# A causal convolution module: the sixth chunk's sum moved behind the eighth chunk's gate, the normalisation's diagonal moved to VectorE, projection copies moved between normalised chunks, and the first norm's squares moved behind its operands

## The chip, the cores and the metric

The kernel runs on one NeuronCore of one Trainium2 chip. The core has a matrix engine (TensorE, PE in the profile; its weight loads are PEld), a vector engine (VectorE, DVE), a scalar engine (ScalarE, ACT), a general engine (GpSimd, POOL), and a queue engine (SyncE, SP) that only starts DMA transfers here. Each engine works through its own list of instructions in order; semaphores tie the lists together. The metric is the time of one execution on the device in microseconds (us), as a median of several executions.

## The reference

Two decoder layers on 512 tokens of width 1024. The change touches only the mixer of the first layer, a causal convolution module, and the norm ahead of it:

```python
def rms_norm(x, g):
    xf = x.astype(jnp.float32)
    y = xf * lax.rsqrt(jnp.mean(xf * xf, axis=-1, keepdims=True) + EPS)
    return (y * g.astype(jnp.float32)).astype(x.dtype)

def conformer_conv(x, w_pw1, b_pw1, dw_w, dw_b, ln_g, ln_b, w_pw2, b_pw2):
    a = x @ w_pw1 + b_pw1
    u = a[..., :D_MODEL] * jax.nn.sigmoid(a[..., D_MODEL:])
    u = lax.conv_general_dilated(u, dw_w[:, None, :], ..., padding=[(30, 0)],
                                 feature_group_count=D_MODEL) + dw_b
    u = jax.nn.silu(layer_norm(u, ln_g, ln_b))
    return u @ w_pw2 + b_pw2
```

The rest of the first layer (a gated feed-forward network and a gated per-layer embedding `gate * (p @ w_proj)`) and the second layer (differential attention, the same two again) are unchanged. One thing of the rest is computed early: the product `p @ w_proj` of the first layer fills PE at the end of the convolution.

## The kernel before

Everything is kept transposed: 1024 features are 8 chunks of 128 partitions, and the 512 tokens run along the free axis, so a tile is 128x512. The input chunks are `h0` to `h7`. Every float32 operand of a matrix product is split into a rounded high part and the low rest, and each product is three matmuls (`mm3`, L164 to L166: low x high, high x low, high x high). A weight tile (`weight`, L146) is loaded by SP, its high part copied on ScalarE (L157), its low part made on VectorE (L159).

*The norm ahead (class `Norm`, L181).* `operands(c)` makes the split operand of a chunk: the high part on ScalarE (L178), the low part on VectorE (L179). `squares(c)` squares the chunk on ScalarE (L200, L203) and adds it on VectorE (L204). `columns` sums over the partitions with four narrow matmuls (L210); the reciprocal root is a power on POOL (L229); `diagonal` puts it on a diagonal (L234, VectorE); `spread` (L244) multiplies that by ones, so that each partition holds the row of scales, which ScalarE copies to `rb` (L219). The products are made of the unscaled operands and scaled behind.

*A chunk of the convolution (loop over c, L459 on).* `half` multiplies by the gate half and the other half of the weights, 24 matmuls each. VectorE scales both by `rb` (L478, L484), ScalarE takes the sigmoid (L479), VectorE joins them (L488 or L496). Then come the 31 taps. Chunks 1, 3, 5 and 6 (counted from 0; `PHASED`) take them all on PE: the joined chunk goes to DRAM and back in another layout (`pi`, L333, L337), PE multiplies by prepared matrices (L370), ScalarE copies the result (L378), it goes to DRAM (`po`, L380, from ScalarE's queue) and back (L383, SP), and VectorE adds bias and the common shift `shrow` (L389). This last step I call the chunk's sum. The other chunks take their taps on VectorE (L419, L421), with some on POOL (L409, products by ScalarE, L408) and, for the eighth chunk (c = 7), eight on PE (L326); VectorE joins the parts (L422, L424). `moments(c)` squares a finished chunk on ScalarE (L444) and adds square and chunk to running sums (L448, L450), on POOL up to the sixth chunk, on VectorE for the seventh. The sum of the seventh chunk is kept back (`late`) until the eighth is done.

*The end.* `factor` makes one of eight chunks of `p @ w_proj`, twelve matmuls (L164 to L166, on `wth`, `wtl`) and a copy on ScalarE (L291). `add_moments` sums squares and values over the partitions (L456) and spreads the mean (L457). Four tiny VectorE operations make the variance (L538 to L227), POOL takes the power, the diagonal is made by four scaled copies on ScalarE (L544), PE spreads it (L547). Each chunk is then shifted by the mean (L555 on VectorE for three, L557 on POOL for five), scaled (L564, VectorE), put through SiLU (L565, ScalarE) and split (L567 ScalarE, L569 VectorE). `linear` multiplies by the second weights, with three output chunks in turn to begin with; L593 adds the result to `h`.

The order on each engine is not written out by hand. A scheduler places the instructions by their dependencies, with its own estimate of times; `tc.issue_after(x)` keeps an instruction behind another one, and `tc.manual_schedule` keeps the written order on the engines that it names. So one move in the code shifts neighbours on all engines.

## Time and profile before

| | |
|---|---|
| median of 3 runs | 1267.42 us (1265.94 to 1268.1) |
| the profiled execution | 1268.78 us |
| its span | 1267.0 us |
| PE busy | 1244.6 us, 98% |
| VectorE, ScalarE, POOL busy | 903.4, 614.7, 263.3 us |
| PE's granted clock, mean | 0.992 of full |

The profile is of one execution. "Busy" counts the time in which an engine carries out an instruction. A row of the timeline gives start, duration, engine, line, operation, the tiles written and read, the shape, and in square brackets the idle time ahead of it with what ended that. Neighbouring instructions of one kind are one row (x16), so its duration is that of all. Matmuls overlap, so the distance of their starts tells more than their durations. The granted clock is what PE's throttle let through, 1.00 being full speed.

### The profile page before, as it was taken

What the parts mean: (1) busy time and instruction counts of PE and PEld (TensorE: products, weight loads), DVE (VectorE), ACT (ScalarE), POOL (GpSimd) and SP (SyncE); (2) the same over time, 40 slices, a digit from 0 to 9 for tenths busy, and PEclk for the clock granted to TensorE, in tenths of its full rate; (3) what the DMA queues carried; (4) which work ended last, traced back from release to release, by engine and by line L of the source; (5) the groups of instructions that cost most, each with busy time, mean ns of one, the idle gap of its engine ahead of it and who ended that gap; (6) DMA issues with size and microseconds to landing.
All of it is one profiled execution on the core that took longest, in us unless ns stands there. A gap on an engine that the chain in (4) does not pass through costs nothing.

```text
span 1267.0 us, 18622 instructions
## 1 busy us (share of the span) xinstructions
PE 1244.6 (98%) x7152; PEld 1089.2 (86%) x7152; DVE 903.4 (71%) x1482; ACT 614.7 (49%) x1023; POOL 263.3 (21%) x231
## 2 busy tenths in 40 slices
PE   9999899999999999999999999999999999999998
PEld 7888678888899889988888978778898999899887
DVE  6997765975588558667678869845965588558665
ACT  6742464542355335456566757734542355235442
POOL 2852522000000000042516633122000000000030
PEclk9999999999999999999999989999999999999999
DMA  7665123474466444243222214213464467444241
GB/s 296 195 194 178 58 68 115 124 184 124 120 176 180 127 124 121 63 145 100 87 93 75 76 42 123 94 51 115 131 162 138 111 175 188 141 105 117 82 133 67
DMA packets 60597, 158.39 MB, mean 125 GB/s; under 512 B 6451, under 2 KB 11059, under 8 KB 60508
## 3 DMA queue, kind: packets, MB, share of 16 engines
q1 hardware_dynamic: 53776, 136.99, 34.3%
q0 software_dynamic: 4608, 16.78, 8.1%
q10 hardware_dynamic: 2124, 3.43, 0.9%
q8 instruction: 56, 0.92, 0.3%
q14 instruction: 33, 0.27, 0.1%
HBM read 151.91 MB, written 4.21 MB: 123 GB/s over the span
## 4 chain that ended last, share of the span: by engine, by line
PE 87%; DVE 6%; DMA 2%; ACT 2%; issue 1%; POOL 1%; SPq 0%; DVEq 0%; ACTq 0%; POOLq 0%
PE mm L164 24%; PE mm L165 24%; PE mm L166 24%; PE tp L166 2%; PE tp L165 2%; PE tp L164 2%; PE sc L165 1%; PE sc L166 1%; PE sc L164 1%; DVE wlo L159 1%; POOL wk L409 1%; DMA po<-big 1%; PE sc L370 1%; PE mm L1006 1%; DVE sc L421 1%
## 5 line engine op out<-in xcount | busy, mean ns | idle before, releaser
L165 PE MATMUL mm<-A,whi 128*128 128x512 f32 (+1 forms) x904 | 311.8, 346 | 1.0 <-DVE A L569 0.7
L164 PE MATMUL mm<-A,wlo 128*128 128x512 f32 (+1 forms) x904 | 308.0, 345 | 3.5 <-ACT A L178 1.8
L166 PE MATMUL mm<-A,whi 128*128 128x512 f32 (+1 forms) x904 | 310.2, 344 | 0.0
L157 ACT CAST whi<-wraw 128x1024 fp32r<-128x1024 f32 (+2 forms) x150 | 151.1, 1015 | 224.5 <-PE mm L166 98.5
L159 DVE TENSOR_TENSOR wlo<-wraw,whi 128x1024 fp32r<-128x1024 f32 (+2 forms) x147 | 185.1, 1262 | 58.4 <-ACT whi L157 58.1
L164 PEld LDWEIGHTS mm<-A,wlo 128*128 128x128 f32 x904 | 171.4, 190 | 25.0 <-ACT A L178 2.7
L165 PEld LDWEIGHTS mm<-A,whi 128*128 128x128 f32 x904 | 171.9, 190 | 22.1 <-issue 1.2
L166 PEld LDWEIGHTS mm<-A,whi 128*128 128x128 f32 x904 | 171.9, 190 | 21.0 <-issue 1.4
L165 PE MATMUL mm<-B,whi 128*128 128x512 f32 x368 | 143.9, 392 | 0.0
L166 PE MATMUL mm<-B,whi 128*128 128x512 f32 x368 | 143.8, 392 | 0.0
L164 PE MATMUL mm<-B,wlo 128*128 128x512 f32 x368 | 141.6, 393 | 0.0
L675 POOL DMA_DIRECT2D C<-in_wts x32 | 28.1, 880 | 511.8 <-DVE h L786 179.0
L204 POOL TENSOR_TENSOR acc<-acc,wk 128x512 f32<-128x512 f32 x35 | 56.4, 1610 | 218.1 <-ACT wk L203 110.7
L166 PEld LDWEIGHTS mm<-B,whi 128*128 128x128 f32 x368 | 69.5, 189 | 15.0
L166 PE MATMUL mm<-whi,A 128*128 128x512 f32 (+1 forms) x224 | 82.0, 367 | 0.0
L164 PEld LDWEIGHTS mm<-B,wlo 128*128 128x128 f32 x368 | 69.5, 189 | 14.3
L165 PEld LDWEIGHTS mm<-B,whi 128*128 128x128 f32 x368 | 69.4, 189 | 14.3
L165 PE MATMUL mm<-wlo,A 128*128 128x512 f32 (+1 forms) x224 | 81.6, 367 | 0.0
L164 PE MATMUL mm<-whi,A 128*128 128x512 f32 (+1 forms) x224 | 81.6, 370 | 0.0
L786 DVE TENSOR_TENSOR h<-mm,h 128x512 f32<-128x512 f32 x48 | 33.0, 687 | 64.6 <-PE mm L166 64.4
L229 POOL TENSOR_TENSOR r<-v,mhalf 128x8 f32<-128x8 f32 (+1 forms) x31 | 45.4, 1465 | 118.4 <-DVE v L227 93.1
L668 DVE TENSOR_TENSOR wlo<-wraw,whi 128x1024 fp32r<-128x1024 f32 x32 | 39.2, 1224 | 31.5 <-ACT whi L667 31.4
(271 smaller groups left out, 2674.2 us busy)
## 6 DMA issues: line engine op xcount, KB each, us to landing
wraw<-in_wts SPq DMA_DIRECT2D x162, 512.0 KB, 3.6
C<-in_wts SPq DMA_DIRECT2D x32, 512.0 KB, 4.8
C<-in_wts POOLq DMA_DIRECT2D x32, 512.0 KB, 6.1
bias<-in_wts SPq DMA_DIRECT2D x32, 256.0 KB, 3.4
wraw<-in_wts SPq DMA_DIRECT2D x16, 384.0 KB, 3.1
D<-in_diag SPq DMA_DIRECT2D x22, 256.0 KB, 4.5
C<-in_diag SPq DMA_DIRECT2D x16, 256.0 KB, 4.7
h<-in_xT SPq DMA_DIRECT2D x8, 256.0 KB, 5.5
```

The source lines that it names most:

```text
L157: A.copy(hi[:, cut], raw[:, cut])
L159: eng.tensor_tensor(lo[:, cut], raw[:, cut], f(hi[:, cut]), ALU.subtract)
L164: T.matmul(acc, al, bh, start=first, stop=False)
L165: T.matmul(acc, ah, bl, start=False, stop=False)
L166: return T.matmul(acc, ah, bh, start=False, stop=last)
L204: self.last = self.eng.tensor_tensor(self.acc, self.acc, sq, ALU.add)
L229: last_pow[0] = G.tensor_tensor(r[:, :n], v[:, :n], mhalf[:, :n], ALU.pow)
L370: last_tap[0] = T.matmul(acc[:, g * P : (g + 1) * P], w, ups[c][:, g, LEAD - m : LEAD - m + P], start=(m == 0), stop=(m == LAGS - 1),)
L409: G.tensor_tensor(pacc, pacc, pr, ALU.add)
L668: V.tensor_tensor(lo, raw, f(hi), ALU.subtract)
L675: nc.gpsimd.dma_start(q, wts[i + 2].rearrange("p (a s) -> p a s", a=2), accum_op=ALU.add)
L786: V.tensor_tensor(h[m], acc, h[m], ALU.add)
```

## The change

Five edits, all in the convolution module or the norm ahead of it:

1. `norm.squares` of all eight chunks go behind the last operand's high part. In the second chunk's gate half, the matmuls of the last four input chunks go behind the column sums; its other half goes behind the spread. The two splits of `p` (L278, L279) go behind the power.
2. The sixth chunk's sum (c = 5) is kept back like the seventh's, until the eighth chunk's gate is joined, and its two additions to the running sums go from POOL to VectorE.
3. The fourth `factor` goes from ahead of the moments to behind them: three, moments, two, spread, three, instead of four, moments, one, spread, three.
4. The diagonal is made by one VectorE product (`diagonal`, as in the norms) instead of four ScalarE copies. The tile `drow` for POOL's shifts is made as soon as the mean is there; VectorE's first shift goes behind the variance, the second and third between the scalings.
5. The low parts of the normalised chunks follow one chunk behind instead of two. The last three `factor` calls stand between the first three normalised chunks on ScalarE. The third weight of `linear` no longer waits for the second scaling.

```diff
-    for c in range(NC):
-        norm.squares(c)
+    with tc.issue_after(norm.scaled.ins):
+        for c in range(NC):
+            norm.squares(c)
...
-    def half(w):
+    def half(w, behind=None, first=0):
         acc = mm()
         for k in range(NC):
-            mm3(acc, wpart(w, k), norm.u[k], k == 0, k == NC - 1)
+            with tc.issue_after(behind.ins) if behind and k >= first else nullcontext():
+                mm3(acc, wpart(w, k), norm.u[k], k == 0, k == NC - 1)
...
-        if c < NC - 2:
+        if c < NC - 3:
             late.pop()()
...
-        eng = G if c < NC - 2 else V
+        eng = G if c < NC - 3 else V
         eng.tensor_tensor(sums["acc"], sums["acc"], sq, ALU.add)
...
-            ph = pfeatures(0, [(sb([P, S], t, 2, F32R), sb([P, S], t, 2, F32R)) for t in ("wth", "wtl")])
+            with tc.issue_after(last_pow[0].ins):
+                ph = pfeatures(0, [(sb([P, S], t, 2, F32R), sb([P, S], t, 2, F32R)) for t in ("wth", "wtl")])
...
-            pg = half(wg)
+            pg = half(wg, norm.summed if c == 1 else None, NC // 2)
...
-            pa = half(wa)
+            pa = half(wa, last_spread[0] if c == 1 else None)
...
-            V.scalar_tensor_tensor(up[:, PAD:], ta, col("b_pw1", c), tg, ALU.add, ALU.mult)
+            gate = V.scalar_tensor_tensor(up[:, PAD:], ta, col("b_pw1", c), tg, ALU.add, ALU.mult)
+        if c == NC - 1:
+            with tc.issue_after(gate.ins):
+                late.pop(0)()
...
-    factor(last_product)
     with tc.issue_after(last_product[0].ins):
         add_moments(y[NC - 1], square, True, False)
         add_moments(macc, sums["acc"], False, True)
-    factor(last_moment)
+    for _ in range(2):
+        factor(last_moment)
+    drow = wk()
+    A.mul(drow, sums["mean"], -1.0 / D)
...
-    dg = wk()
-    for b in range(4):
-        A.activation(dg[:, b * P : (b + 1) * P], ident, AF.Copy, scale=r[:, b : b + 1])
+    shift = lambda c: V.scalar_tensor_tensor(y[c], sums["mean"], -1.0 / D, y[c], ALU.mult, ALU.add)
+    with tc.issue_after(last_v[0].ins):
+        shift(0)
+    dg = diagonal(r)
...
-    for _ in range(3):
-        factor(last_product)
     with tc.issue_after(last_pow[0].ins):
-        drow = wk()
-        A.mul(drow, sums["mean"], -1.0 / D)
-        for c in range(NC):
-            if c < 3:
-                V.scalar_tensor_tensor(y[c], sums["mean"], -1.0 / D, y[c], ALU.mult, ALU.add)
-            else:
-                G.tensor_tensor(y[c], y[c], drow, ALU.add)
+        for c in range(3, NC):
+            G.tensor_tensor(y[c], y[c], drow, ALU.add)
...
-        for c in range(NC + 2):
+        for c in range(NC + 1):
             if c < NC:
-                scaled.append(V.tensor_tensor(y[c], y[c], lrow, ALU.mult))
+                if c in (1, 2):
+                    shift(c)
+                V.tensor_tensor(y[c], y[c], lrow, ALU.mult)
...
+                if c < 3:
+                    factor(last_product)
-            if c >= 2:
-                V.tensor_tensor(z[c - 2][1], y[c - 2], f(z[c - 2][0]), ALU.subtract)
+            if c >= 1:
+                V.tensor_tensor(z[c - 1][1], y[c - 1], f(z[c - 1][0]), ALU.subtract)
...
-    linear(NC, z, add_conv, 3, first=(None, last_add[0], scaled[1]))
+    linear(NC, z, add_conv, 3, first=(None, last_add[0], None))
```

What the scheduler makes of it is shown at three places. The changed kernel's line numbers are up to 12 higher than those of the kernel before.

VectorE around the eighth chunk's gate, before. `B_210` is the sixth chunk, `C_225` the eighth behind its gate, `sc_1253` its tap sum, `B_240` the finished eighth chunk:

```order
L421 SCALAR_TENSOR_TENSOR sc_847<-C_159_794,C_24_125,sc_847 128x512 x7
L422 TENSOR_TENSOR B_187_920<-sc_847,wk_888 128x512
L478 TENSOR_TENSOR big_1193<-mm_1090,rb_252 128x512
L159 TENSOR_TENSOR wlo_1464<-wraw_1462,whi_1463 128x1024
...
L389 SCALAR_TENSOR_TENSOR B_210_1080<-B_210_1080,vec_63,shrow_189 128x512
L484 TENSOR_TENSOR big_1194<-mm_1115,rb_252 128x512
L496 SCALAR_TENSOR_TENSOR C_225_1200<-big_1194,vec_63,big_1193 128x512
L419 SCALAR_TENSOR_TENSOR sc_1253<-C_225_1200,C_24_125,shrow_189 128x512
L421 SCALAR_TENSOR_TENSOR sc_1253<-C_225_1200,C_24_125,sc_1253 128x512 x14
L422 TENSOR_TENSOR B_240_1252<-sc_1253,wk_1229 128x512
```

The same place now:

```order
L426 SCALAR_TENSOR_TENSOR sc_847<-C_159_794,C_24_125,sc_847 128x512 x6
L427 TENSOR_TENSOR B_187_920<-sc_847,wk_888 128x512
L484 TENSOR_TENSOR big_1192<-mm_1089,rb_252 128x512
L159 TENSOR_TENSOR wlo_1461<-wraw_1459,whi_1460 128x1024
...
L490 TENSOR_TENSOR big_1193<-mm_1114,rb_252 128x512
L502 SCALAR_TENSOR_TENSOR C_225_1199<-big_1193,vec_63,big_1192 128x512
L394 SCALAR_TENSOR_TENSOR B_210_1080<-B_210_1080,vec_63,shrow_189 128x512
L424 SCALAR_TENSOR_TENSOR sc_1253<-C_225_1199,C_24_125,shrow_189 128x512
L455 TENSOR_TENSOR acc_190<-acc_190,B_210_1080 128x512
L426 SCALAR_TENSOR_TENSOR sc_1253<-C_225_1199,C_24_125,sc_1253 128x512 x3
L453 TENSOR_TENSOR B_93_381<-B_93_381,wk_1272 128x512
L426 SCALAR_TENSOR_TENSOR sc_1253<-C_225_1199,C_24_125,sc_1253 128x512 x11
```

The sixth chunk's sum (L389, now L394) has moved behind the gate, but still stands ahead of the taps, and two additions stand among the taps. The fifth chunk's last run of taps has six where it had seven (the other one stands earlier).

ScalarE at the head, before (`h_7` to `h_14` are the eight input chunks, `A` their operands):

```order
L157 CAST whi_96<-wraw_95 128x512
L178 ACTIVATE A_19_105<-h_7_86,vec_63 128x512
L200 ACTIVATE acc_94<-h_7_86 128x512
L157 CAST whi_96<-wraw_95 128x512
L157 CAST whi_110<-wraw_109 128x512
L178 ACTIVATE A_25_127<-h_8_87,vec_63 128x512
L203 ACTIVATE wk_168<-h_8_87 128x512
```

and now:

```order
L157 CAST whi_96<-wraw_95 128x512
L178 ACTIVATE A_19_105<-h_7_86,vec_63 128x512
L157 CAST whi_96<-wraw_95 128x512
L157 CAST whi_110<-wraw_109 128x512
L178 ACTIVATE A_25_127<-h_8_87,vec_63 128x512
L157 CAST whi_110<-wraw_109 128x512
L178 ACTIVATE A_27_131<-h_9_88,vec_63 128x512
```

The squares have left the places between the operands; they follow the eighth operand.

ScalarE at the end, before (`D`, `C_270` are projection chunks, `B_93`, `B_115`, `B_140` the first three chunks, `A_274`, `A_276` their high parts):

```order
L291 COPY D_259_1323<-mm_1324 128x512
L157 CAST whi_1475<-wraw_1474 128x1024
L291 COPY D_261_1350<-mm_1351 128x512
L544 ACTIVATE wk_1367<-ident_65,r_265_1365 128x128 x4
L552 ACTIVATE wk_1400<-tp_1288 128x512
L291 COPY D_268_1374<-mm_1375 128x512
L565 ACTIVATE B_93_381<-B_93_381,vec_63 128x512
L291 COPY C_270_1383<-mm_1384 128x512
L567 CAST A_274_1414<-B_93_381 128x512
L565 ACTIVATE B_115_536<-B_115_536,vec_63 128x512
L291 COPY C_270_1383<-mm_1392 128x512
L157 CAST whi_1578<-wraw_1577 128x1024
```

and now:

```order
L546 ACTIVATE wk_1359<-tp_1288 128x512
L295 COPY D_259_1341<-mm_1342 128x512
L157 CAST whi_1472<-wraw_1471 128x1024
L295 COPY D_261_1350<-mm_1351 128x512
L571 ACTIVATE B_93_381<-B_93_381,vec_63 128x512
L573 CAST A_269_1383<-B_93_381 128x512
L295 COPY D_271_1386<-mm_1387 128x512
L571 ACTIVATE B_115_536<-B_115_536,vec_63 128x512
L573 CAST A_273_1398<-B_115_536 128x512
L295 COPY C_275_1401<-mm_1402 128x512
L157 CAST whi_1575<-wraw_1574 128x1024
L571 ACTIVATE B_140_652<-B_140_652,vec_63 128x512
```

The four scaled copies are gone, the copy of the mean stands earlier, and each of the last three projection copies stands behind a normalised chunk's high part.

11 lines of the change are left out of this document (6 added, 5 removed).

## The prediction

> **What bounds the kernel now.** I read the page first: how busy is TensorE (PE), and where is it not?
>
> ```profile
> span 1267.0 us, 18622 instructions
> PE 1244.6 (98%) x7152; PEld 1089.2 (86%) x7152; DVE 903.4 (71%) x1482; ACT 614.7 (49%) x1023; POOL 263.3 (21%) x231
> ```
>
> PE is idle for 22.4 us in all. The windows, by 20 us and finer, show where the convolution's share lies (the stretch and its length, then the busy time of PE, weight loads, VectorE, ScalarE and POOL, then PE's granted clock, DMA share and GB/s):
>
> ```profile
> 60.00:80.00 20.00, 20.00 (x115) 17.19 (x114) 19.18 (x23) 9.18 (x13) 7.06 (x7) 1.00 0.61 176
> 140.00:160.00 20.00, 16.51 (x76) 12.29 (x75) 12.95 (x20) 8.07 (x16) 8.69 (x7) 0.91 0.14 39
> ...
> 8.00:12.00 4.00, 4.00 (x12) 3.10 (x12) 4.00 (x7) 3.95 (x8) 0.00 (x0) 0.57 1.06 401
> ...
> 156.00:158.00 2.00, 2.00 (x7) 1.52 (x6) 2.00 (x4) 0.00 (x0) 2.00 (x2) 0.50 0.00 0
> ...
> 700.00:750.00 50.00, 47.60 (x284) 42.09 (x283) 41.09 (x114) 34.95 (x85) 26.40 (x26) 0.93 0.25 74
> ```
>
> In the convolution there are two holes: the head, where the clock was 0.57 of full from 8 to 12 us, and 140 to 165 us, its end, where it fell to 0.50. (The last row is in the attention, where PE waits as well.) In between PE is full (20.00 of 20), and VectorE (19.18) nearly so. What ends the waits of the second hole is in PE's timeline (the last row is from the chain of waits, an earlier spread at full clock):
>
> ```profile
> 143.97 0.50 PE L164 MATMUL mm<-wth,wlo 128*128 128x512 f32 x1 [1.64 <-DVE B L424]
> 145.47 0.95 PE L456 MATMUL tp<-ones,wk 128*128 128x1 f32 x8
> 150.67 0.48 PE L164 MATMUL mm<-wth,wlo 128*128 128x512 f32 x1
> 154.15 1.47 PE L547 MATMUL tp<-wk,ones 128*128 128x512 f32 x2 [1.85 <-ACT wk L544]
> 158.32 0.39 PE L165 MATMUL mm<-wth,whi 128*128 128x512 f32 x1
> 160.61 0.39 PE L166 MATMUL mm<-wtl,whi 128*128 128x512 f32 x1
> 162.49 0.50 PE L165 MATMUL mm<-A,whi 128*128 128x512 f32 x1 [0.70 <-DVE A L569]
> ...
> 28.10 0.86 PE tp L244 x2
> ```
>
> PE waits 1.64 us for the eighth chunk's sum (L424), 1.85 for the diagonal that ScalarE makes (L544), 0.70 for the first normalised chunk. At full clock a matmul starts every 0.229 us (158.32 to 160.61, ten steps); from 154.15 to 158.32 it does one spread and seven matmuls, which at that pace are 0.86 + 7 x 0.229 = 2.46 us: the half clock behind the 1.85 us wait costs 1.7. The output projection, had it not waited, would stand at 162.49 less its three first matmuls, 161.80. That mark is what the change must pull in; behind it PE is the bound, so the end follows it.
>
> What makes L424 late is in VectorE's timeline (the first row is PE's, the first tap of the seventh chunk, which follows the last matmul of the eighth chunk's halves):
>
> ```profile
> 123.16 3.06 PE L370 MATMUL mm<-C,D 128*128 128x128 f32 x26
> ...
> 127.16 1.12 DVE L389 SCALAR_TENSOR_TENSOR B<-B,vec,shrow 128x512 f32<-128x512 f32 x1 [4.64 <-DMA B<-po]
> 128.19 0.68 DVE L484 TENSOR_TENSOR big<-mm,rb 128x512 f32<-128x512 f32 x1
> 128.91 1.33 DVE L496 SCALAR_TENSOR_TENSOR C<-big,vec,big 128x512 f32<-128x512 f32 x1
> 131.14 11.05 DVE L421 SCALAR_TENSOR_TENSOR sc<-C,C,sc 128x512 f32<-128x512 f32 x14
> 142.43 0.69 DVE L422 TENSOR_TENSOR B<-sc,wk 128x512 f32<-128x512 f32 x1 [0.24 <-POOL wk L409]
> 143.23 0.69 DVE L424 TENSOR_TENSOR B<-mm,B 128x512 f32<-128x512 f32 x1
> ```
>
> VectorE stands 4.64 us until the sixth chunk's rows land, and the eighth chunk's gate (L484, L496) stands behind that wait though PE had its input ready at 123.2.
>
> **The change part by part.**
>
> *Head.* ScalarE loses the square between the first operand and the next weight copies:
>
> ```profile
> 5.36 0.62 ACT L200 ACTIVATE acc<-h 128x512 f32<-128x512 f32 x1
> 7.78 1.03 PE L164 MATMUL mm<-A,wlo 128*128 128x512 f32 x2 [0.76 <-ACT A L178]
> 18.75 1.93 DVE L159 TENSOR_TENSOR wlo<-wraw,whi 128x1024 fp32r<-128x1024 f32 x1 [0.30 <-ACT whi L157]
> 19.73 0.95 PE L210 MATMUL tp<-ones,acc 128*128 128x1 f32 x8
> 25.67 1.23 DVE L159 TENSOR_TENSOR wlo<-wraw,whi 128x1024 fp32r<-128x1024 f32 x1 [2.12 <-ACT whi L157]
> 29.61 0.69 DVE L478 TENSOR_TENSOR big<-mm,rb 128x512 f32<-128x512 f32 x1 [2.72 <-ACT rb L219]
> ```
>
> That brings the operand for which PE waits at 7.78 forward by most of 0.62; I take 0.5. From 8 us on PE waits for no operand (4.00 of 4 busy), so the other squares' place only gives slack. The eight squares and their sums are the old instructions in a new order; with the weight splits among them both engines were through at 18.75 + 1.93 = 20.7. The column sums now stand twelve matmuls (2.75 us) further, at 19.2 + 2.75 = 22.0, so they wait for nothing. The row scale is spread after twelve more, at 22.0 + 0.8 + 2.75 = 25.5; with 0.86 for the spread and about 0.7 for the copy behind it, VectorE's first gate starts near 27.1 instead of 29.61. One weight split (1.23, at 25.67 inside that wait) moves behind it, so VectorE is about 1.3 us ahead from there. PE needs that split only for the third chunk, a whole chunk later. On POOL the two splits of the projection's input go behind the first power, which would cost them if POOL had other work; its next is a tap of the first chunk, after the gate. On SP's queue a load for the FFN falls back behind the second chunk's matrices, which nobody waits for; otherwise neighbours change places.
>
> *Sixth chunk's rows.* Their trip begins with a copy on ScalarE behind the fifth chunk's square, which waits for VectorE:
>
> ```profile
> 116.65 0.69 DVE L422 TENSOR_TENSOR B<-sc,wk 128x512 f32<-128x512 f32 x1
> 117.91 0.57 ACT L378 COPY big<-sc 128x512 f32<-128x512 f32 x1
> ```
>
> If VectorE keeps its 1.3 us and has one tap fewer ahead of L422 (the order shows six for seven), the rows land up to 2 us earlier. If the fourth chunk's trip, whose copy now stands one product later, eats it, 0. I take 1.0, the middle.
>
> *Eighth chunk.* Off the path from landing to L424: L484 and L496, 128.91 + 1.33 - 128.19 = 2.05, which run in the former wait, and POOL's 0.24, since its taps start with the gate; together 2.29. On it: the two additions of the sixth chunk to the running sums (L450, L448), which come from POOL to VectorE. Their price alone, then the prices of two operations next to POOL (L569 and L389; L389 alone is above) and that of taps of two chunks in turn:
>
> ```profile
> 146.02 0.69 DVE L450 TENSOR_TENSOR acc<-acc,B 128x512 f32<-128x512 f32 x1
> 160.82 1.62 DVE L569 TENSOR_TENSOR A<-B,A 128x512 fp32r<-128x512 f32 x1 [0.73 <-ACT A L567]
> 84.51 4.04 DVE L421 SCALAR_TENSOR_TENSOR sc<-C,C,sc 128x512 f32<-128x512 f32 x6
> 93.70 2.02 DVE L389 SCALAR_TENSOR_TENSOR B<-B,vec,shrow 128x512 f32<-128x512 f32 x1 [1.38 <-DMA B<-po]
> ```
>
> Alone two adds are 1.38. Taps of one chunk follow each other at 11.05 / 14 = 0.79, taps of two chunks in turn at 4.04 / 6 = 0.67, so an add between two taps gets 0.12 back, 0.24 in all. Next to POOL's seven taps, which now start some 4 us earlier, they could cost 1.62 each, and L389 2.02 instead of 1.12. So this segment changes by -2.29 + 1.38 - 0.24 = -1.15 to -2.29 + 3.24 - 0.24 + 0.90 = +1.6. I take +0.2, the middle, since neither row is nearer: POOL works through all of it, but not always in the same microsecond. L424 then ends at 143.92 - 1.0 + 0.2 = 143.12.
>
> *Moments.* The fourth projection no longer stands ahead of them. They start when the eighth chunk is squared:
>
> ```profile
> 143.95 0.64 ACT L444 ACTIVATE wk<-B 128x512 f32<-128x512 f32 x1 [1.00 <-DVE B L424]
> ```
>
> That is 0.67 after L424: 143.79. PE is free at 143.97 - 1.64 - 0.5 = 141.83, so it waits 1.96. The moments take 150.67 - 145.47 = 5.20 and end at 148.99 (call it E).
>
> *Diagonal and spread.* The four scaled copies (L544) become one VectorE product, priced as an equal one at 22.86:
>
> ```profile
> 151.69 1.02 POOL L229 TENSOR_TENSOR r<-v,mhalf 128x4 f32<-128x4 f32 x1 [9.29 <-DVE v L227]
> 22.86 0.69 DVE L234 TENSOR_TENSOR wk<-ident,r 128x512 f32<-128x512 f32 x1 [1.98 <-POOL r L229]
> ```
>
> POOL's power ends at 152.71, E + 2.04; the diagonal at E + 2.8 (VectorE does the first shift while POOL works). PE meanwhile has two projections, 12 x 0.229 = 2.75. The 1.85 us wait is thus covered, up to 0.6 if POOL's shifts double the diagonal's price. Spread 0.86 and three projections 4.12 bring the output projection to E + 7.78 = 156.77. Gain against 161.80: 5.0 us.
>
> *Normalised chunks.* They pass VectorE and ScalarE in turn:
>
> ```profile
> 160.68 0.82 ACT L565 ACTIVATE B<-B,vec 128x512 f32<-128x512 f32 x1
> 162.81 0.62 ACT L567 CAST A<-B 128x512 fp32r<-128x512 f32 x1
> ```
>
> The first one's low part is due at E + 2.04 + 0.69 (diagonal) + 1.23 (the third weight's split, now ahead of it) + 0.69 (product) + 0.82 (SiLU) + 0.62 + 0.69 (difference) = E + 6.8, with hand-overs some E + 7.3; next to POOL the two-input ones would take it to about E + 8.9. PE comes to it two matmuls into the output projection, at E + 8.2. I charge 0.3, bounds 0 and 0.7. The projection copies, now later on ScalarE, free PE's banks for the second and third weight about an instruction ahead of need.
>
> *Clock.* A wait of 1.64 cost no clock, one of 1.85 cost 1.7 us. The new wait of 1.96 is near that edge: 0 to 1.7, and I take 0.85. [...]
>
> **Sum.** 5.0 - 0.3 - 0.85 = 3.9 us. The profiled execution (1268.78, 1267.0 of it span) becomes 1264.9. It was 1.36 above the median; from the median 1267.42 I predict 1263.5. Two medians closer than 0.2%, 2.5 us, count as the same here.
>
> **The rivals.**
>
> *The new sums are dear.* POOL stays beside VectorE for both adds and L389 (+1.6) and the rows land no earlier. The rows of L569 and L389 next to POOL speak for it; against it, an add may meet a gap between POOL's taps. The moments start at 143.92 + 1.6 + 0.67 = 146.19 after a wait of 4.4, the clock drops (1.7), E = 153.09, the mark 161.17 with 0.3: gain 0.6, 1266.8. [...]
>
> [...]
>
> *Head without half clock.* Less waiting before 8 us may spare the drop there: 4 x (1 - 0.57) = 1.7 more, 1261.8. Nothing in the trace says which.
>
> *Given back later.* Attention has PE waits too, and shifted times may cost one more stretch at half clock: 3.9 - 1.7 = 2.2, 1265.2, about on the 0.2% line.
>
> *Slower: the sixth chunk's rows land late.* All fifteen taps of the eighth chunk stand on VectorE behind L389, so each us of landing beyond 126.2 is a us at the end. The fourth chunk's trip began, in the chain, at
>
> ```profile
> 83.18 0.57 ACT big L378
> ```
>
> The rival decides from 3.9 us late (130.1); at 133, 6.8 late, the kernel takes 1270.3. For it: the trip passes ScalarE's copy, a store, and SP's queue behind the matrix loads. Against: from its copy to VectorE's L389 the fourth chunk's trip took 93.70 - 83.18 = 10.5 and the sixth's 127.16 - 117.91 = 9.3, a spread of 1.2, not 7.
>
> **How the numbers follow.** Forecast 0.42; clock held 0.14; head without half clock 0.09; dear sums 0.19; given back 0.10, half to either side of the line; late rows 0.06. Faster 0.42 + 0.14 + 0.09 + 0.05 = 0.70; same 0.19 + 0.05 = 0.24; slower 0.06. The range runs from the head case with 1 us of the sixth chunk's bound, 1260.8, to the dear sums, 1266.8.
>
> **What would show it.** In the changed profile: the eighth gate starts near 123 and its C tile is written before the sixth chunk's rows land; the wait for the eighth chunk's sum is 1 to 3 us and no longer behind a fourth projection; no wait of 1.85 at the spread; the output projection begins near 156.8. I am wrong if VectorE's adds there take over 1.3 us each, if PE's clock halves for over 4 us, or if a new wait stands ahead of the output projection's second or third weight.

## The result, and the profile after

The changed kernel takes 1272.27 us (median of 7 executions, 1269.98 to 1273.69), the kernel before beside it 1267.42 (7 executions): a ratio of 1.0036, 95% interval 1.0025 to 1.0047. It is 4.9 us slower where 3.9 us less was forecast, and lies outside the range. Measured again on another chip it took 1273.12 us, 1.0030 of the kernel before (1.0010 to 1.0051). Three executions below took 1.6 to 5 times as long as all others (3172.59 us of the kernel before, 6719.67 of *adds on GpSimd*, 2059.47 of *wait filled, shifts behind*): the medians count them, the ratios leave them out.

Lines behind the edits have moved: L389 is now L394, L419 to L424 are L424 to L429, L444 to L457 are L449 to L462, L484 and L496 are L490 and L502. The profiled execution took 1269.98 us, the shortest of the seven. The head came out as forecast. These are the column sums, the spread, ScalarE's copy of the row and VectorE's first gate:

```profile
21.58 0.95 PE L211 MATMUL tp<-ones,acc 128*128 128x1 f32 x8
25.80 1.10 PE L247 MATMUL tp<-wk,ones 128*128 128x512 f32 x2 [0.39 <-DVE wk L235]
26.94 0.59 ACT L220 COPY rb<-tp 128x512 f32<-128x512 f32 x1 [6.84 <-PE tp L247]
27.56 0.69 DVE L484 TENSOR_TENSOR big<-mm,rb 128x512 f32<-128x512 f32 x1 [1.90 <-ACT rb L220]
```

22.0, 25.5 and 27.1 were forecast for the sums, the spread and the gate, and they started at 21.58, 25.80 and 27.56. The next place did not come out so. ScalarE's queue, with the sixth chunk's copy and its store:

```profile
116.54 0.57 ACT L383 COPY big<-sc 128x512 f32<-128x512 f32 x1
119.13 0.33 ACTq L385 DMA_DIRECT2D po<-big  x1
119.55 1.05 ACT L157 CAST whi<-wraw 128x1024 fp32r<-128x1024 f32 x1 [2.44 <-DMA C<-pi]
```

The copy is 1.4 us earlier than before (117.91), yet the store stands 2.0 us behind its end: the profile names a DMA, `C<-pi`, the seventh chunk's reload, as what the cast behind the store, and so ScalarE's queue, waited for. The records of the trace show the tie between the two: store and reload raise the same completion semaphore, the reload's last piece landed at 119.05, and the store started at 119.13. (In the kernel before, 118.58 and 118.66.) So the rows land 0.53 us later than before. VectorE from the eighth chunk's gate to its last sum, and then the diagonal:

```profile
122.99 0.69 DVE L490 TENSOR_TENSOR big<-mm,rb 128x512 f32<-128x512 f32 x1
123.72 0.75 DVE L502 SCALAR_TENSOR_TENSOR C<-big,vec,big 128x512 f32<-128x512 f32 x1
127.69 1.85 DVE L394 SCALAR_TENSOR_TENSOR B<-B,vec,shrow 128x512 f32<-128x512 f32 x1 [3.22 <-DMA B<-po]
129.46 1.73 DVE L424 SCALAR_TENSOR_TENSOR sc<-C,C,shrow 128x512 f32<-128x512 f32 x1
131.10 1.76 DVE L455 TENSOR_TENSOR acc<-acc,B 128x512 f32<-128x512 f32 x1
132.78 2.33 DVE L426 SCALAR_TENSOR_TENSOR sc<-C,C,sc 128x512 f32<-128x512 f32 x3
135.01 0.86 DVE L453 TENSOR_TENSOR B<-B,wk 128x512 f32<-128x512 f32 x1
135.80 8.66 DVE L426 SCALAR_TENSOR_TENSOR sc<-C,C,sc 128x512 f32<-128x512 f32 x11
144.56 0.69 DVE L427 TENSOR_TENSOR B<-sc,wk 128x512 f32<-128x512 f32 x1
145.36 0.69 DVE L429 TENSOR_TENSOR B<-mm,B 128x512 f32<-128x512 f32 x1
...
157.78 1.77 DVE L235 TENSOR_TENSOR wk<-ident,r 128x512 f32<-128x512 f32 x1 [0.55 <-POOL r L230]
```

The gate runs inside the wait for the rows, as forecast. But next to POOL's taps the sum, the first tap and the first addition take 1.85, 1.73 and 1.76 us, where the kernel before had 1.12 and 0.76 for the first two and 0.69 alone for such an addition. The second addition, beside the same taps, takes only 0.86. From landing to the end of the last sum it is 18.36 us against 16.76. PE's waits at the end of the convolution:

```profile
146.77 1.87 PE L461 MATMUL tp<-ones,wk 128*128 128x1 f32 x8 [4.80 <-ACT wk L449]
...
154.82 1.03 PE L461 MATMUL tp<-ones,acc 128*128 128x1 f32 x8
159.70 1.10 PE L559 MATMUL tp<-wk,ones 128*128 128x512 f32 x2 [1.02 <-DVE wk L235]
164.74 0.62 PE L164 MATMUL mm<-A,wlo 128*128 128x512 f32 x2
```

PE waits 4.80 us for the eighth chunk, where the kernel before waited 1.64. The moments, 5.20 us before, last from 146.77 to 155.71, 8.94 us. The windows show why (as before: busy times, then the granted clock):

```profile
140.61:144.03 3.42, 1.35 (x6) 0.78 (x5) 3.28 (x5) 1.18 (x2) 0.00 (x0) 1.00 0.00 0
144.03:147.44 3.41, 0.67 (x4) 0.67 (x4) 3.20 (x5) 0.97 (x2) 0.00 (x0) 0.50 0.00 0
147.44:150.85 3.41, 3.41 (x15) 3.25 (x16) 1.96 (x3) 0.28 (x1) 0.00 (x0) 0.50 0.42 127
150.85:154.27 3.42, 3.42 (x8) 1.52 (x6) 0.00 (x0) 0.27 (x1) 0.00 (x0) 0.50 0.07 26
154.27:157.68 3.41, 3.41 (x23) 3.09 (x24) 1.25 (x5) 0.65 (x2) 0.95 (x1) 1.00 0.00 0
```

The clock is at half for 10.24 us, three stretches of 3.41. The output projection starts at 164.74, 2.94 later than the mark of before. These 2.94 are 1.30 (moments begin later) + 3.74 (moments longer) - 2.10 (from their end to the output projection: 9.03 against 11.13).

### The profile page after: what moved, and what is told of

It is laid out like the page before. It is cut to its first block, busy times and chain, and to the rows that moved or that the text cites. A ratio compares the mean times of both kernels' runs of the same rounds, so it can differ in the third digit from the quotient of the medians.

```text
span 1268.2 us, 18626 instructions
## 1 busy us (share of the span) xinstructions
PE 1243.5 (98%) x7152; PEld 1088.4 (86%) x7152; DVE 909.2 (72%) x1485; ACT 614.5 (48%) x1019; POOL 264.1 (21%) x229
## 4 chain that ended last, share of the span: by engine, by line
PE 81%; DVE 8%; issue 6%; ACT 2%; POOL 2%; DMA 1%; ACTq 0%; SPq 0%; POOLq 0%; DVEq 0%
PE mm L164 22%; PE mm L165 22%; PE mm L166 22%; PE tp L166 2%; PE tp L165 2%; PE tp L164 2%; DVE wlo L159 1%; POOL wk L414 1%; DVE sc L426 1%; PE sc L165 1%; PE sc L166 1%; PE sc L164 1%; PE mm L1014 1%; DVE C L951 1%; DVE big L990 0%
## 5 line engine op out<-in xcount | busy, mean ns | idle before, releaser
L159 DVE TENSOR_TENSOR wlo<-wraw,whi 128x1024 fp32r<-128x1024 f32 (+2 forms) x147 | 185.9, 1267 | 60.8 <-ACT whi L157 60.6
```

The source lines that it names most:

```text
L159: eng.tensor_tensor(lo[:, cut], raw[:, cut], f(hi[:, cut]), ALU.subtract)
```

## The experiments

Theory 1, from the two traces: the eighth chunk's chain is longer, mostly by the two sums on VectorE next to POOL's taps, and the longer wait that follows costs TensorE's clock in the moments. Rival 1: the loss lies in the diagonal on VectorE and the normalised chunks. Rival 2: it lies behind the convolution.

Every kernel was timed in five rounds beside the kernel before (its medians 1266.35 to 1266.86), in 12 executions each, *fourth projection ahead* in six. Four chips were used: one for the second to fifth row of the table, one for the next four, one for the first row and the three of the small fill, one for the last four. So kernels of different chips are compared by their ratios, not by their microseconds. The matmuls that fill waits are extra work that nothing reads. "Clock" is the mean granted clock over the executions; the kernel before had 0.995 (0.989 to 0.998), the changed one 0.992 in both measurements.

| kernel | us | ratio to before | clock, lowest |
|---|---|---|---|
| changed, again | 1273.12 | 1.0030 (1.0010 to 1.0051) | 0.992, 0.989 |
| sums back | 1267.23 | 1.0003 (0.9990 to 1.0016) | 0.994, 0.990 |
| wait filled | 1267.51 | 1.0005 (0.9996 to 1.0015) | 0.996, 0.993 |
| fourth projection ahead | 1274.43 | 1.0049 (1.0034 to 1.0064) | 0.991, 0.989 |
| only the sums | 1271.21 | 1.0032 (1.0019 to 1.0046) | 0.992, 0.989 |
| adds on GpSimd | 1267.06 | 1.0005 (0.9989 to 1.0021) | 0.993, 0.988 |
| the same, both waits filled | 1267.09 | 1.0005 (0.9995 to 1.0016) | 0.996, 0.995 |
| before, waits filled | 1268.07 | 1.0006 (0.9993 to 1.0020) | 0.996, 0.994 |
| wait filled, shifts behind | 1266.38 | 0.9995 (0.9981 to 1.0010) | 0.996, 0.990 |
| adds, small fill | 1268.77 | 1.0015 (0.9997 to 1.0033) | 0.993, 0.989 |
| the same, shifts behind | 1269.49 | 1.0007 (0.9989 to 1.0025) | 0.993, 0.990 |
| the same, store free | 1267.97 | 1.0010 (0.9992 to 1.0028) | 0.994, 0.990 |
| adds, wide fill | 1266.51 | 0.9996 (0.9983 to 1.0008) | 0.996, 0.993 |
| row first, filled | 1264.77 | 0.9984 (0.9972 to 0.9997) | 0.994, 0.992 |
| row first | 1264.74 | 0.9985 (0.9972 to 0.9997) | 0.994, 0.992 |
| row first, store free | 1265.12 | 0.9992 (0.9978 to 1.0005) | 0.993, 0.990 |

**Which part costs it.** *Sums back*, from the changed kernel:

```diff
-        if c < NC - 3:
+        if c < NC - 2:
             late.pop()()
...
-        eng = G if c < NC - 3 else V
+        eng = G if c < NC - 2 else V
...
-        if c == NC - 1:
-            with tc.issue_after(gate.ins):
-                late.pop(0)()
```

> The changed kernel with one part taken back: the sixth chunk's sum stands ahead of the eighth chunk's gate again and its two running sums are on GpSimd. Theory 1 (the eighth chunk's chain and the clock behind it): the two sums cost VectorE about 1.6 us next to GpSimd's taps, and the moments lose 3.7 us at half clock because TensorE waits 4.80 us ahead of them. Here the eighth chunk's last sum should end near 144.4 us instead of 146.05, the wait should be near 3.1 us, and the time should fall by 1.6 us if the half clock stays and by up to 5.3 us if the shorter wait keeps the clock: 1267.0 to 1270.7 us against 1272.3. Rival 1 (the loss lies in the diagonal on VectorE and the normalised chunks): the last sum's end moves but the output projection gains at most 1.6 us. Rival 2 (the loss lies behind the convolution): the output projection starts earlier, and the whole time stays at 1272.

1267.23 us, a ratio of 1.0003 in place of 1.0036 and 1.0030: some 3.4 to 4.2 us of the loss are gone, inside theory 1's range. The loss of clock is rarer here, not gone. Six of 12 executions reach a clock of 0.995, against six of 19 of the changed kernel. The profiled one is this kernel's slowest (1272.37): its stretch from landing to last sum is 16.98 us, PE waits 3.28, and four stretches at half clock follow.

```profile
146.29 1.05 PE L461 MATMUL tp<-ones,wk 128*128 128x1 f32 x8 [3.28 <-ACT wk L449]
```

*Only the sums* is the kernel before with the opposite edit and nothing else:

> The kernel before with one part of the change alone: the sixth chunk's sum behind the eighth's gate and its two running sums on VectorE. Theory 1: the eighth chunk's last sum ends 1.6 us later than in the kernel before (143.9), near 145.5; TensorE waits near 3.2 us instead of 1.64; with the full clock kept the time rises by 1.6 us, with the clock lost by up to 5 us: 1269 to 1272.5 against 1267.4. Rival 1: this part costs nothing by itself: 1267.4, or up to 2 us less since the gate no longer waits.

1271.21 us: this part alone makes the loss, 1.0032 against the whole change's 1.0030 and 1.0036. Its mean clock is 0.992 against 0.995, and 0.003 of 1268 us is 3.8 us, nearly all of the loss. Rival 1 falls; so does rival 2 as a cause, since no code behind the convolution differs here. The other edits together are worth about nothing as they stand. In its trace the stretch from landing to last sum is 18.49 us, but the rows landed at 125.54, so the wait came out at 2.12, not 3.2. It stands right ahead of the moments, as in the changed kernel, although the fourth projection was not moved in the code: the scheduler now has PE do it ahead of the wait.

```profile
144.74 1.05 PE L456 MATMUL tp<-ones,wk 128*128 128x1 f32 x8 [2.12 <-ACT wk L444]
```

Two stretches at half clock follow, one in the moments and one behind the spread.

**Is it the wait?** *Wait filled*, from the changed kernel (`spare` is the unused rest of the PSUM tile of the column sums; the lines that keep the moments in their order are left out here):

```diff
     with tc.issue_after(last_product[0].ins):
+        for _ in range(18):
+            last_product[0] = T.matmul(spare[:, 8:S], wpart(pw[0], 0)[0], ph[0][0][:, 8:], start=True, stop=True)
+    with tc.issue_after(last_product[0].ins):
         add_moments(y[NC - 1], square, True, False)
```

> The changed kernel with 18 matmuls put on TensorE between the third projection and the moments, whose results nothing reads; no other engine's order changes. They take about 0.22 us each, 4.0 us, and lie in a wait of 4.80 us. Theory 1: the moments keep the full clock and take 5.2 us instead of 8.94, the output projection starts near 161.0 us instead of 164.74, and the time falls by 3.7 us to about 1268.5. Rivals 1 and 2: the clock of the moments isn't set by the wait, or doesn't decide the end: no change within 1 us.

PE's rows, the fill, the moments and the output projection:

```profile
141.30 4.26 PE L543 MATMUL tp<-wth,whi 128*128 128x504 f32 x18
145.40 0.95 PE L462 MATMUL tp<-ones,wk 128*128 128x1 f32 x8
149.71 1.03 PE L462 MATMUL tp<-ones,acc 128*128 128x1 f32 x8
150.60 0.48 PE L164 MATMUL mm<-wth,wlo 128*128 128x512 f32 x1
...
159.66 0.62 PE L164 MATMUL mm<-A,wlo 128*128 128x512 f32 x2
```

The moments take 5.20 us again (145.40 to 150.60), and useless work brings the ratio from 1.0036 and 1.0030 down to 1.0005, 3.2 to 3.9 us: the loss is the clock. Theory 1 expected 3.7. *Fourth projection ahead* fills part of the wait with real work:

```diff
+    factor(last_product)
     with tc.issue_after(last_product[0].ins):
         add_moments(y[NC - 1], square, True, False)
         add_moments(macc, sums["acc"], False, True)
-    for _ in range(2):
-        factor(last_moment)
+    factor(last_moment)
```

> The changed kernel with the fourth projection ahead of the moments again (one projection, not two, between them and the spread). Theory 1: the wait ahead of the moments falls from 4.80 to 3.4 us; the half clock gets shorter or goes, so that the output projection starts 0 to 3.7 us earlier, and the time is 1268.5 to 1272.3. Rival 1: a wait of 1 to 2.4 us comes back ahead of the spread of the normalisation, and nothing is gained: 1272.3 or up to 1.4 us more.

It missed: 1274.43, a ratio of 1.0049 and so no better than the changed kernel, although the wait fell to 2.12 us. It also lies above the rival's 1273.7, and the wait ahead of the spread, 1.07 us, is the changed kernel's (1.02). (The scheduler also moved some neighbours in the attention.) Its windows from the wait on:

```profile
144.78:148.19 3.41, 1.29 (x12) 1.19 (x11) 3.29 (x4) 1.49 (x3) 0.00 (x0) 1.00 0.00 0
148.19:151.60 3.41, 3.41 (x10) 2.34 (x10) 2.58 (x4) 1.19 (x2) 0.00 (x0) 0.50 0.54 153
...
161.84:165.26 3.42, 3.42 (x9) 2.56 (x8) 2.75 (x4) 1.86 (x3) 3.04 (x3) 0.50 0.00 0
```

A shorter wait, and five stretches at half clock, most of them with PE busy throughout. So "the wait" was not the whole theory. *Before, waits filled* (7 matmuls ahead of the fourth projection and 7 ahead of the spread):

```diff
+    for _ in range(7):
+        with tc.issue_after(last_product[0].ins):
+            last_product[0] = T.matmul(spare[:, 8:S], ...)
     factor(last_product)
...
+    for _ in range(7):
+        with tc.issue_after(last_product[0].ins):
+            last_product[0] = T.matmul(spare[:, 8:S], ...)
     with tc.issue_after(last_product[0].ins):
         last_product[0] = T.matmul(lrow, ones, dg, start=True, stop=True)
```

> The kernel before with 7 matmuls that nothing reads in each of its two waits, ahead of the fourth projection (1.64 us) and ahead of the spread (1.85 us). If the kernel before loses clock there only in some executions (its mean clock ran from 0.992 to 0.998 over 29 runs), the mean falls by 0.5 to 1.5 us and the upper times go: 1265 to 1266. If its waits cost it nothing in most executions: 1266.4, unchanged, or up to 0.3 us more for the matmuls.

1268.07 us, 1.0006 of before: no gain, so what clock the kernel before loses here is not worth the fill.

**Why the chain is longer.** *Adds on GpSimd* keeps the sum behind the gate and gives the two additions back (`eng = G if c < NC - 2 else V`):

> The changed kernel with the sixth chunk's two running sums on GpSimd again, and its sum still behind the eighth chunk's gate. Theory 1 (the two sums on VectorE next to GpSimd's taps are what lengthens the eighth chunk's chain): they took 1.76 and 0.86 us there, so the stretch from the landing of the sixth chunk's rows to the eighth chunk's last sum is 15.8 to 16.2 us instead of 18.36, and TensorE's wait ahead of the moments falls from 4.80 to about 2.4 us; the time falls by 2.4 us, and by up to 6 if the clock holds: 1266 to 1270 against 1272.3. Rival (the taps next to GpSimd take the time whichever engine adds, and GpSimd with two more sums ends its taps late): the stretch stays above 17.5 us, and the time within 1 us of 1272.3.

VectorE's rows, with the stretch from landing to last sum:

```profile
127.30 1.12 DVE L394 SCALAR_TENSOR_TENSOR B<-B,vec,shrow 128x512 f32<-128x512 f32 x1 [3.28 <-DMA B<-po]
128.33 0.76 DVE L424 SCALAR_TENSOR_TENSOR sc<-C,C,shrow 128x512 f32<-128x512 f32 x1
129.12 11.05 DVE L426 SCALAR_TENSOR_TENSOR sc<-C,C,sc 128x512 f32<-128x512 f32 x14
140.76 0.69 DVE L427 TENSOR_TENSOR B<-sc,wk 128x512 f32<-128x512 f32 x1 [0.59 <-POOL wk L414]
141.56 0.69 DVE L429 TENSOR_TENSOR B<-mm,B 128x512 f32<-128x512 f32 x1
```

The stretch is 14.95 us, less than theory 1's 15.8: not only the additions go, the sum and the first tap are back at 1.12 and 0.76 too, since GpSimd's addition must wait for the sum and its taps stand behind that addition (they start at 130.17 instead of 126.07). PE waited 1.45 us, the clock held, the output projection started at 157.33 (forecast for the changed kernel: 156.77), and this execution took 1262.54. But the median is 1267.06: six of the 12 executions have a clock under 0.995, down to 0.988.

*The same, both waits filled* (12 wide matmuls ahead of the moments, 4 ahead of the spread):

> The same, with 12 matmuls that nothing reads ahead of the moments and 4 ahead of the spread of the normalisation, to fill both waits. Theory 1 (the clock is lost to the waits, the rest of the loss to the sums): the moments take 5.2 us, no stretch at half clock lies between 140 and 165 us, the output projection starts near 157.5 us, and the time is 1264.5 to 1266, up to 2 us under the kernel before's 1266.4. Rival (what is won at the output projection is given back behind it, as the first filled kernel's 1267.5 may say): 1266.5 to 1267.5 with the output projection as early as that.

The clock is back (no execution under 0.995), the time is not: 12 matmuls are 2.75 us, more than the wait, and the output projection starts at 159.11, not near 157.5, with waits of 0.27 us ahead of it and 0.60 in it for a normalised chunk. So the expected 1264.5 to 1266 was missed.

*Wait filled, shifts behind* puts a small GpSimd instruction that reads the diagonal ahead of its five shifts:

```diff
     with tc.issue_after(last_pow[0].ins):
+        tiny = sb([P, P // 2], "v8", 2)[:, :8]
+        seen = G.tensor_tensor(tiny[:, :4], dg[:, :4], mhalf[:, :4], ALU.add)
+    with tc.issue_after(seen.ins):
         for c in range(3, NC):
             G.tensor_tensor(y[c], y[c], drow, ALU.add)
```

> The changed kernel with the 18 filling matmuls ahead of the moments, and GpSimd's five shifts behind the diagonal instead of beside it (a small GpSimd instruction that reads the diagonal stands ahead of them). Theory (the diagonal's 1.77 us is contention with the shifts): the diagonal takes 0.69 us, the wait of 1.03 us ahead of the spread goes, and the output projection starts near 158.6 instead of 159.66 us; the time falls from 1267.5 by up to 1.0. Rival (the shifts are needed as early as they are): a normalised chunk waits for its shift, the output projection starts no earlier or waits behind its first matmuls, and the time is 1267.5 or more.

The diagonal on VectorE, alone:

```profile
152.36 0.69 DVE L235 TENSOR_TENSOR wk<-ident,r 128x512 f32<-128x512 f32 x1 [0.54 <-POOL r L230]
```

0.69 us instead of 1.77, and no wait ahead of the spread; the output projection starts at 158.23 instead of 159.66, 1.1 us nearer to the end of the moments. The median is 1.1 us lower than that of the fill alone, measured on another chip and with intervals that overlap.

**Wait or streaming?** The first try at a fitting fill used 24 matmuls of 128 columns on *adds on GpSimd* (`spare[:, P : 2 * P]`, `ph[0][0][:, :P]`):

> The changed kernel with the sixth chunk's two running sums on GpSimd and, ahead of the moments, 24 small matmuls (128 columns, some 0.06 us each, 1.4 us in all) that nothing reads; no other instruction changes place. In the execution profiled without them TensorE waited 1.45 us there, the clock held, the output projection started at 157.33 us and the time was 1262.5, but the median was 1266.7. Theory 1 (what keeps the other executions above that one is clock lost to this wait and the one of 1.02 us behind it): with the wait filled the median falls to about 1263 to 1264.5 and the mean clock stays at 0.995 or more. Rival (the lost clock of those executions lies in the attention, not here): the median stays at 1266 to 1267.

They took 0.11 us each, not the 0.06 that would be a quarter of the 0.229 of 512 columns, so the fill was too long; and in the profiled execution, the slowest of the 12, the clock was lost with no wait at all. The fill, and the windows:

```profile
144.40 2.79 PE L543 MATMUL tp<-wth,whi 128*128 128x128 f32 x24
```

```profile
141.46:144.87 3.41, 3.41 (x19) 2.89 (x18) 2.74 (x4) 1.45 (x3) 1.29 (x1) 1.00 0.00 0
144.87:148.29 3.42, 3.42 (x33) 3.42 (x32) 2.80 (x4) 1.36 (x3) 0.00 (x0) 1.00 0.18 31
148.29:151.70 3.41, 3.41 (x9) 2.10 (x9) 0.00 (x0) 0.00 (x0) 0.00 (x0) 0.50 0.31 123
```

PE was busy for 3.42 of 3.42 us from 144.87, yet the next four stretches ran at half clock. What that stretch held was 128-column and one-column matmuls, 33 of them, where 3.42 us hold 15 of 512 columns at 0.229 us each: busy by the profile, which models the ends of matmuls, but with little streamed. Theory 2, a guess formed here from this one stretch: the clock goes where few columns are streamed, under one-column matmuls as in a wait. *Shifts behind* and *store free* were run on the same fill and carry its cost:

> The same, with GpSimd's five shifts behind the diagonal. Theory (contention made the diagonal 1.77 us): the diagonal takes 0.69 us, TensorE waits for nothing ahead of the spread, and the time falls by another 1.0 us, to 1262 to 1263.5. Rival: a normalised chunk now waits for its shift, and the time is that of the kernel without this edit.

1269.49 us, no faster than the 1268.77 without the edit, as the rival has it. Both carry the fill, and only four of 12 executions of each reach a clock of 0.995, so this does not say that the shifts are needed early. But its profiled execution, with the same fill and no wait either, keeps the clock through the fill (145.66 to 148.29) and the moments:

```profile
144.43:147.85 3.42, 3.42 (x28) 3.19 (x26) 3.42 (x5) 2.23 (x4) 0.00 (x0) 1.00 0.00 0
147.85:151.26 3.41, 3.41 (x25) 2.85 (x25) 0.43 (x1) 0.00 (x0) 0.00 (x0) 1.00 0.50 154
```

So behind the same narrow work one execution lost the clock and another kept it. Perhaps it matters what falls into one stretch of 3.41 us: the one from 144.87, which half clock followed, held narrow matmuls alone, and these two also hold wide ones. No run tests that. *Store free* has fewer transfers between the reload and the store, so that the two no longer raise the same semaphore:

```diff
-                for m in range(2):
-                    nc.sync.dma_start(two[m], diag[i + 2 * g + m])
+                nc.sync.dma_start(both_, diag[i + 2 * g : i + 2 * g + 2].rearrange("m p a b -> p m a b"))
...
-                with after_weights(c):
+                with tc.issue_after(rows_in[NC - 3].ins) if c == NC - 1 else after_weights(c):
                     nc.sync.dma_start(dg[:, :n], diag[TAPS.index((c, j)), :, :n])
```

(`rows_in[c]` is the last load of a chunk's rows.)

> The same once more, with fewer DMAs between the fifth chunk's reload and the sixth chunk's store, so that the store of the sixth chunk's rows no longer waits for a reload of the seventh chunk: the two matrices that lie side by side in one tile are loaded by one DMA instead of two, and a matrix of the eighth chunk is loaded behind the sixth chunk's rows. Theory (the store stood 1.5 us behind its copy for that reload alone): it is issued at 117.0 instead of 118.6 us, the rows land near 125.8 instead of 127.3, and the output projection starts up to 1.5 us earlier: 1261 to 1262. Rival (the store's 5 us go into DMA queues that are full at that time): it is issued earlier and lands when it did, or TensorE waits for the late matrix; no gain, or up to 1 us lost.

ScalarE's store and VectorE's sum in its trace (its lines stand one lower: L382, L384 and L393 for L383, L385 and L394):

```profile
116.01 0.57 ACT L382 COPY big<-sc 128x512 f32<-128x512 f32 x1
116.60 0.33 ACTq L384 DMA_DIRECT2D po<-big  x1
```

```profile
124.40 1.15 DVE L393 SCALAR_TENSOR_TENSOR B<-B,vec,shrow 128x512 f32<-128x512 f32 x1 [0.38 <-DMA B<-po]
```

The store follows its copy at once, and the rows land 3.3 us earlier than in the changed kernel. Of these 3.3 us the copy's earlier start makes 0.5 and the wait 2.0. So the reload was what held it. The time, 1267.97, missed the expected 1261 to 1262; it again has the fill in it.

*Changed, again* is the changed kernel on the chip of these three:

> The changed kernel as it is, beside the other three on the same chip. Theory 1: 1271 to 1273 us with a mean clock of 0.990 to 0.994, a wait near 4.8 us ahead of the moments, and two to five stretches at half clock behind it. Rival (the first result was the chip's): within 2 us of the kernel before.

As theory 1 says: its trace has a wait of 4.37 us and two stretches at half clock behind it. Its executions fall into two groups, five at 1267.96 to 1271.04 (clock 0.995 or 0.996) and seven at 1272.75 to 1275.79 (0.989 to 0.992).

*Wide fill* is the direct test of theory 2: 12 matmuls of 504 columns in place of the 24 of 128.

> The changed kernel with the two running sums on GpSimd and 12 matmuls of 504 columns ahead of the moments, 2.75 us, as long as the 24 matmuls of 128 columns that took 2.8 us in the kernel measured at 1268.8 with a mean clock down to 0.989. Nothing else differs from that kernel. Theory 2 (streamed columns count): the clock holds, mean clock 0.995 or more in nearly all executions, 1266 to 1267. Theory 1 (only a wait counts, and neither kernel waits): the same time and clock as with the small ones, 1268.8 and down to 0.989.

The fill, and the clock of the moments (143.96 to 149.2) in the windows:

```profile
141.23 2.90 PE L543 MATMUL tp<-wth,whi 128*128 128x504 f32 x12
```

```profile
143.80:147.20 3.40, 3.40 (x22) 2.65 (x21) 0.91 (x2) 0.00 (x0) 0.00 (x0) 1.00 0.52 154
147.20:150.60 3.40, 3.40 (x23) 2.94 (x23) 1.15 (x5) 0.60 (x1) 0.41 (x1) 1.00 0.00 0
```

Equal time for the fill, the same moments behind it, and the clock holds: 10 of 12 executions at 0.995 or more against 4 of 12 with the small fill. The times, 1266.51 and 1268.77 on two chips, point the same way; their ratios' intervals overlap. Part of the difference may be the chip: the kernel before reached 0.995 in 26 of 35 executions beside the wide fill, and in 19 of 35 beside the small one. So theory 2 is made likely, not shown.

**A version that uses it.** *Row first* begins the moments with the 512-column row of the eighth chunk, which needs no square; its additions are on GpSimd and the shifts behind the diagonal. `add_moments` no longer holds its wide matmul:

```diff
     with tc.issue_after(last_product[0].ins):
+        row = T.matmul(sums["mean"], ones, y[NC - 1], start=True, stop=False)
+    with tc.issue_after(row.ins):
         add_moments(y[NC - 1], square, True, False)
+    with tc.issue_after(last_moment[0].ins):
+        row = T.matmul(sums["mean"], ones, macc, start=False, stop=True)
+    with tc.issue_after(row.ins):
         add_moments(macc, sums["acc"], False, True)
```

> The same without the 3 matmuls: a wait near 0.75 us is left ahead of the row. Both theories: the clock holds in most executions, 1263 to 1265.5. Rival as above: 1267 to 1269.

With three wide matmuls ahead of the row:

> The changed kernel with the sixth chunk's two running sums on GpSimd, GpSimd's shifts behind the diagonal, the moments begun with the 512-column row of the eighth chunk (it needs only the chunk, not its square, and so can start some 0.7 us earlier), and 3 wide matmuls that nothing reads ahead of it (0.7 us). Theory 2 (the clock goes where little is streamed through TensorE for a stretch of the throttle, in waits and one-column matmuls alike): no more than 2 us of one-column matmuls now stand together, the clock holds, the mean clock is 0.995 or more in nearly all executions, and the time is 1263 to 1265. Theory 1 (the wait alone counts): the same here. Rival (the clock of this place is lost whatever stands there): mean clock down to 0.990 in a third of the executions, 1267 to 1269.

1264.74 and 1264.77 us, 0.9985 and 0.9984 of before (at most 0.9997): about 2 us faster than the kernel before, and by the ratios some 5.7 to 6.5 us faster than the changed one. The rival's 1267 to 1269 falls. Theory 2's clock is only half met: no execution is under 0.992, but six of 12 (filled) and three of 12 (not) reach 0.995; one stretch at half clock behind the moments is left in both traces. Filling the last 0.7 us changes nothing.

*Row first, store free*:

> The same, without filling matmuls, with the free store of the sixth chunk's rows: in the execution profiled with it the rows landed at 124.4 us, 3 us earlier, and the eighth chunk's last sum ended at 139.3, ahead of TensorE's third projection at 141.4. Here the row of the eighth chunk then follows the projections with no wait, the output projection starts near 154.5 us in an execution without a half-clock stretch, and the time is 1260 to 1262.5: faster than both kernels. Rival (given back behind the output projection, or the clock lost as before): 1265 to 1267.

1265.12: the rival's case. In its trace the store started at 117.97, 0.74 us behind its copy: the DMA that raised the same semaphore before it was now a load of a matrix, whose last piece landed at 117.89. So the rows landed at 126.27, not at 124.4. PE had no wait ahead of the row, and the clock fell for two stretches in and behind the moments. Earlier rows did not help here, where the clock was lost with no wait ahead of the row.

## Why the prediction was wrong, point by point

*Head.* Right in its times (above), and worth nothing at the end: PE's first tap of the seventh chunk stood at 122.79, and at 122.09 in *only the sums*, whose head is the old one and whose first microseconds ran at full clock. The 123.16 of before had a half-clock stretch in it (0.57 from 8 to 12 us). The changed profile has none there, as the rival "head without half clock" asked; but five of the 15 traces with the new head do have one, and two of the three with the old, so this looks like the execution's luck.

*Sixth chunk's rows* (-1.0, bounds 0 to 2). Failed by 1.5 us in the profiled execution: the copy is earlier as forecast, the store is not, because it waits in ScalarE's queue for the seventh chunk's reload. The prediction followed engines and SP's queue, not the DMA that a DMA waits for; *store free* shows it. How long it waits differs between executions: in *wait filled*, whose order up to here is the same, the reload was done at 117.63 and the rows landed at 126.09, as forecast (126.16).

*Eighth chunk* (+0.2, between -1.15 and +1.6). It came out at the upper bound, +1.6, in part by other terms: the first addition cost 1.7 and the second 0.8, together less than the bound's 3.24, but the first tap, which the prediction put at nothing, cost 0.85 more. The rival "the new sums are dear" had this and the rows that land no earlier; it ended at 1266.8 because it priced the clock at 1.7. The middle was the wrong choice: the sum, the first tap and the first addition stand right where POOL's taps begin (126.07), and took 1.73 to 1.85 us there against 0.69 to 1.12 without POOL beside them. Not every operation is held up: the later taps kept 0.78 us beside the same POOL taps, which run to 137.01, and the second addition took 0.86. Why these and not those was not shown.

*Moments.* They start at 146.77, not 143.79: 1.5 by the rows, 1.4 by the chain.

*Clock* (0.85, between 0 and 1.7). This is the step that turned the sign. 3.74 us were lost in the profiled execution; *wait filled* takes them away. The bound was taken from one stretch behind a wait of 1.85 us, but the wait came out at 4.80 instead of 1.96 (so the case that the clock holds, with the chance 0.14, 5.0 - 0.3 = 4.7 us gained and 1262.7, did not come), and it stands next to the moments' one-column matmuls, where the kernel before had its fourth projection between the two (six matmuls by its rows, not the twelve given for `factor` above). (*Only the sums* and *fourth projection ahead* have the wait there too, behind a fourth projection, so the third edit alone is not the reason.) Stretches followed one another, up to five (*fourth projection ahead*). Half clock came in stretches of 3.41 us and its multiples: 3.41 us behind the wait of 1.85 in the kernel before (154.80 to 158.21), 10.24 here, 17.07 in *fourth projection ahead*. The length of a wait alone does not decide it here: the clock fell behind a wait of 2.12 us, and with PE busy 3.42 of 3.42, and one wait of 2.09 us in the attention (L970, now L978) lies at half clock in part in the kernel before (0.66 from 730 to 740 us) and at full clock in the changed one (1.00).

*Diagonal and spread* (7.78 from the moments' end). 9.03. The diagonal took 1.77 us beside POOL's shifts and left a wait of 1.02; *shifts behind* took both away. The prediction had named this as up to 0.6.

*Normalised chunks* (0.3). No wait; nothing was lost.

*The sum.* Against the forecast of 1264.9 for the profiled execution: rows and chain 2.98, clock 3.74 - 0.85 = 2.89, diagonal 1.25 - 0.3 = 0.95, together 6.82 at the output projection. Behind it 1.74 came back, since the spans differ by 1.2 and the marks by 2.94: 6.82 - 1.74 = 5.08, and 1269.98 - 1264.9 is 5.08. The 1.74 are in part luck: the execution of before had three stretches at half clock in the attention, the changed one only one (clock 0.93 and 1.00 from 700 to 750 us). Two stretches are worth 2 x 3.41 x 0.5 = 3.4 us, so something else behind the mark cost 1.7; what, stays open. The medians lie further apart than the two profiles, because the one execution was among the better of its kernel and the other (clock 0.992 against a mean of 0.995) among the worse.

What stays open: what of PE's work decides whether the clock holds, and why one execution loses the clock where another of the same kernel keeps it. One wide and one narrow fill tell the direction, not the measure. Why *row first* keeps a half-clock stretch was not tried further either.

## What to carry to other kernels

Look for stretches in which TensorE is busy with very narrow matmuls, and count them with the waits beside them: a wait right ahead of narrow work cost up to five stretches at half clock here (*fourth projection ahead*), by estimate 5 x 3.41 x 0.5 = 8.5 us behind a wait of 2.12. Wide work put between the two, or begun with, is worth a try. Before an instruction is moved next to another engine's work, price it by a row of its own form beside that engine, and take that end of the bound if the two start together. For a transfer's start, ask also which earlier DMA its queue waits for; here it was the one that raised the same semaphore, and the store stood 2.0 us for it.

## What the runs showed of the hardware

- A 128-column matmul of the filling kind took 0.11 us (24 in 2.79, *adds, small fill*), half as much as one with 504 columns (18 in 4.26, 0.23 each, *wait filled*).
- Half clock lasted over PE-busy time: five stretches of 3.41 us behind a wait of 2.12 us, PE busy throughout four of them (*fourth projection ahead*).
- The executions of one kernel spread with their clock: the changed kernel from 1267.96 to 1275.79 us, with clocks from 0.996 to 0.989 (*changed, again*, 12 executions).
- The store of the sixth chunk's rows started 0.07 to 0.08 us behind the last piece of an earlier transfer that raises the same completion semaphore, in four traces (119.05 and 119.13 in the changed kernel, 118.58 and 118.66 before, 117.63 and 117.70 with the wait filled, 117.89 and 117.97 in *row first, store free*). In *store free*, where the reload does not raise it, the store started at 116.60, 0.02 us behind the end of its copy.
